# Moving the start addresses of a fused two-block transformer kernel's operand pools with small unused tiles

## The chip, the cores and the metric

The kernel runs on one core of a Trainium2 chip. The metric is the device time of one execution in microseconds (us); three timed executions are summed up by their median. One further execution was profiled, and the rows below are from that one. On-chip memory (SBUF) has 128 partitions; an address here is a byte offset within a partition, the same in all 128. TensorE (PE) takes two operands of a matmul from SBUF: the stationary one ("weights" of the array, loaded by a LDWEIGHTS that the profile lists under PEld) and the moving one, which streams through.

## What is computed

Two transformer blocks for one sequence of 512 tokens with 1024 features, all in float32. Cut to its outline:

```python
def first_block(x, c, ...):              # 2 layers, modulated by c
    for layer in range(2):
        mod = silu(c) @ ada_w[layer] + ada_b[layer]        # shift, scale, gate, twice
        h = rmsnorm(x, g) * (1 + scale_m) + shift_m
        y = gdn_mixer(h, ...) if layer == 0 else mla_mixer(h, ...)
        x = x + gate_m * y
        h = rmsnorm(x, g) * (1 + scale_f) + shift_f
        x = x + gate_f * ((silu(h @ w_gate) * (h @ w_up)) @ w_down)
    return rmsnorm(x, final_norm_g)

def second_block(x, ...):                # retention and window attention side by side
    h = rms_norm(x, ln1)
    proj = h @ w_in + b_in               # 1024 -> 6400 columns
    branch_a = (silu(rg) * head_norm(retention(rq, rk, rv))) @ w_ret_out
    branch_b = window_attention(aq, ak, av) @ w_attn_out
    x = x + (sigmoid(gate_a) * branch_a + sigmoid(gate_b) * branch_b) @ w_out
    x = x + swiglu(rms_norm(x, ln2))
    return rms_norm(x, lnf)
```

`gdn_mixer` is a chunked gated delta rule with 8 heads, `mla_mixer` is latent attention with 8 heads.

## The kernel before

**Products.** Nearly every large product is made three times in the format float32r, with both operands split into a high and a low part: high by high, low by high and high by low (`mm3`, L140 to L143). The stationary operand is a 128x128 piece of a weight matrix (`whi`, `wlo`), the moving one 512 or 256 tokens of an activation. In a few places (the values of attention and of retention) the roles are exchanged: the activation is loaded and the weights stream. A panel of weights (128 partitions x 1024 numbers) arrives by one DMA in `wraw`, ScalarE (ACT) copies its high part to `whi` (L566), and VectorE (DVE), in places GpSimd (POOL), subtracts to give `wlo` (L567). The stages run one after the other: the start, `gdn`, `ffn(0)`, `mla`, `ffn(1)`, `block2`, `ffn(2)`; `residual` closes each and prepares the first products of the next. Attention and the delta rule also use plain float32 matmuls, each of which shows as two records.

**Order.** PE's order is the order of the code, since PE is scheduled by hand (L335) with fillers between the chains (`Loom`). The other engines' queues are ordered by the scheduler of the language.

**Pools.** All tiles lie in pools that are stacked one behind the other, in the order in which they are opened. `Net.__init__` opens `cst` (constants), `sm` (small statistics), `adp`, `hp` (the split input of a stage, `hhi` and `hlo`, by `hpair`, L625) and `xp` (the residual stream). After `gdn`, `nm`, `wr` (`wraw`) and `wp` (`whi`, `wlo`) follow, and then each stage's own: `ffa` and `ffs` of `ffn` (`ah`, `al`, and `far`, `fsg`), `mla` of `mla`, `b2`, `b2c`, `b2s` of `block2`. The pools of `gdn` itself (`gh`, `gt` and others) are stacked from the other end. Two tiles hold more room than they use: `ones` (L377, 200 numbers more) and `lev` (L986, 24 more). In the built program `hp`, `xp`, `nm`, `wr`, `wp`, `ffa`, `ffs`, `mla` and `b2` begin at a multiple of 256 bytes, and so does every tile of 2048 or 4096 bytes in them. So each float32r matmul has its moving and its stationary operand at 0 mod 256, but for the 24 matmuls into `abps` of the start, whose stationary operand is 16 columns wide (64 bytes): the first and fifth three read it at 0, the other eighteen at 64, 128 and 192 mod 256. Elsewhere the start differs: `c_sq` (the identity and the masks) begins at 160 mod 256, `ones` at 128, and `rS`, the moving state of retention (L1469), at 96.

Of the kernel before, what the change touches and what calls it, by code (L numbers as in the profile page):

```python
# [12 lines left out]
F32 = mybir.dt.float32  # L13
# [7 lines left out]
P = 128  # L21
# [110 lines left out]


END = object()
Q3 = 0.65
LANES = 3
HALF = (slice(0, T // 2), slice(T // 2, T))
# [8 lines left out]
class Loom:  # L146
# [7 lines left out]
    def run(self, chains, filler, side=None, every=4):  # L154
        at = {g: self.t for g in chains}
        count, tries = 0, 0
        while at:
            ready = [g for g in at if at[g] <= self.t]
            for g in ready:
                if at[g] > self.t:  # L160
                    continue
                r = next(g, END)
                if r is END:
                    del at[g]
# [3 lines left out]
            if ready:  # L168
                continue
            c = next(filler, END)  # L170
            if c is END or c is None:
                self.t = max(self.t, min(at.values()))
# [151 lines left out]
class Net:  # L324
    def __init__(self, tc, I, es):
        self.tc, self.nc, self.I, self.es = tc, tc.nc, I, es
        self.cst = self.pool("cst", 1, es)
        self.sm = self.pool("sm", 4, es)
        self.adp = self.pool("adp", 1, es)
        self.hp = self.pool("hp", 8, es)  # L330
        self.xp = self.pool("xp", KD, es)
        self.pp = self.pool("pp", 3, es, space=PSUM)
        self.sp = self.pool("sp", 5, es, space=PSUM)
        self.wide, self.turn, self.lopool, self.behind = False, 0, False, None
        es.enter_context(tc.manual_schedule(engines={mybir.EngineType.PE}))  # L335

    def pool(self, name, bufs, es, **k):
        if k.get("space") is None:
            k["reuse_waits"] = "tile"
        return es.enter_context(self.tc.tile_pool(name=name, bufs=bufs, **k))  # L340

    def weights(self, es, n, **k):

# [3 lines left out]
    def first(self, gen, offset=300):  # L347

        while True:
            with self.tc.high_priority(offset=offset):  # L350
                r = next(gen, END)
            if r is END:
                return
# [252 lines left out]
    def stream(self, specs):  # L606

        nxt = specs[0][0]()
        for i, (_, h, done, *when) in enumerate(specs):
# [4 lines left out]
            for k, _ in enumerate(h(ps, wt) if callable(h) else self.proj(ps, wt, h)):  # L614
                if k == min(1, n - 1) and i + 1 < len(specs):
                    nxt = specs[i + 1][0]()
                if k < n - 1:
                    yield Q3
            done(ps)
            yield Q3  # L620

# [547 lines left out]
    def ffn(self, l, before, first, gate, norm, firsts, side=None):  # L1169
        nc, h = self.nc, before.h  # L1170
        wg, wu, wd = self.ffn_weights(l)
        with ExitStack() as es:
            fa, fs = self.pool("ffa", 8, es), self.pool("ffs", 2, es)
            sg, a = {}, None

            def gate_done(c):
                def done(ps):
                    sg[c] = fs.tile([P, T], F32, name="fsg")
                    if before.late:
                        nc.vector.tensor_tensor(sg[c], ps, before.row, op=ALU.mult)  # L1180
                        nc.scalar.activation(sg[c], sg[c], AF.Silu)  # L1181
                        nc.gpsimd.tensor_tensor(sg[c], sg[c], before.row, op=ALU.mult)  # L1182
                    else:
                        nc.scalar.activation(sg[c], ps, AF.Silu)
                return done

            def up_done(c, a):
                def done(ps):
                    ar = fs.tile([P, T], F32, name="far")
                    self.behind = nc.vector.tensor_tensor(ar, ps, sg.pop(c), op=ALU.mult).ins  # L1190
                    ah, al = fa.tile([P, T], F32R, name="ah"), fa.tile([P, T], F32R, name="al")
                    self.split(ah, al, ar)
                    a[0].append(ah)
                    a[1].append(al)
                return done
            specs = []
            for g, (lo, hi) in enumerate(FGROUPS):
                a = ([], [])
                for c in range(lo, hi):
                    specs += [(self.w(wg, c * P), h, gate_done(c)), (self.w(wu, c * P), h, up_done(c, a))]  # L1200
                if g < len(FGROUPS) - 1:
                    for n in range(KD):
                        specs.append((self.w(wd.rows(lo, hi), n * P), a, lambda ps, n=n: self.add_to_x(n, ps, gate)))
            for (_, _, done), ps in zip(specs, first):
                done(ps)
            for n, _ in enumerate(self.stream(specs[len(first):])):
                if side is not None and n % 5 == 0:
                    next(side, None)
            if side is not None:
                drain(side)  # L1210
                self.rope_tables(lambda name: self.nm.tile([P, T], F32, name=name, tag="sq", bufs=3))
            norm = norm()
            return norm, self.residual(wd.rows(lo, hi), a, gate, norm, firsts)
# [79 lines left out]
    def mla(self, h, first, gate, norm, firsts):  # L1293
        nc, I, sm = self.nc, self.I, self.sm
        scale = 192.0 ** -0.5
        with ExitStack() as es:
            mp = self.pool("mla", 37, es)
            t = lambda name: mp.tile([P, T], F32, name=name, tag="m")
            tr = lambda name: mp.tile([P, T], F32R, name=name, tag="m")
# [130 lines left out]
            f = fill()  # L1430
# [129 lines left out]
    def block2(self, before, first, norm, firsts):  # L1560
        nc, I, sm, h = self.nc, self.I, self.sm, before.h
        w = self.W("w_in_2")
        with ExitStack() as es:
            mp = self.pool("b2", 35, es)
            t = lambda name: mp.tile([P, T], F32, name=name, tag="m")
            tr = lambda name: mp.tile([P, T], F32R, name=name, tag="m")
# [172 lines left out]
            f = self.stream(specs)  # L1739
# [111 lines left out]
```

## Time and profile before

| | |
|---|---|
| median of three runs | 2292.67 us (2290.30 to 2297.39) |
| the profiled execution | 2289.49 us |
| its span, first to last instruction | 2287.7 us |
| PE busy | 2190.1 us, 96% |
| weight loads (PEld) busy | 1845.3 us, 81% |
| DVE, ACT, POOL busy | 1296.7, 875.5, 405.7 us |
| DMA, mean rate | 113 GB/s |

A busy time is the union of an engine's instructions. A matmul's record is longer than the time by which the next one follows it, since they are pipelined; so the cost of one in a stream is read from the starts of neighbours, not from its duration. The granted clock of TensorE has two levels here, full (2.4 GHz, written 1.00) and half (1.2 GHz, written 0.50); a value between them is a mixture within the stretch.

### The profile page before, as it was taken

What the parts mean: (1) busy time and instruction counts of PE and PEld (TensorE: products, weight loads), DVE (VectorE), ACT (ScalarE), POOL (GpSimd) and SP (SyncE); (2) the same over time, 40 slices, a digit from 0 to 9 for tenths busy, and PEclk for the clock granted to TensorE, in tenths of its full rate; (3) what the DMA queues carried; (4) which work ended last, traced back from release to release, by engine and by line L of the source; (5) the groups of instructions that cost most, each with busy time, mean ns of one, the idle gap of its engine ahead of it and who ended that gap; (6) DMA issues with size and microseconds to landing.
All of it is one profiled execution on the core that took longest, in us unless ns stands there. A gap on an engine that the chain in (4) does not pass through costs nothing.

```text
span 2287.7 us, 30713 instructions
## 1 busy us (share of the span) xinstructions
PE 2190.1 (96%) x11532; PEld 1845.3 (81%) x11532; DVE 1296.7 (57%) x2845; ACT 875.5 (38%) x1950; POOL 405.7 (18%) x331
## 2 busy tenths in 40 slices
PE   6999868899999999999999999999999999999998
PEld 4787767788888897679888888888778789888888
DVE  7888677577663356655433336665655655433334
ACT  4664355343222244434323234233544633322223
POOL 5345554120000031012000002212111002101011
PEclk7999888999999999999999999999999999999999
DMA  7233344248763313122332323433323141433332
GB/s 274 70 97 123 102 156 154 70 141 271 251 229 106 92 56 93 45 66 65 114 102 88 106 88 97 139 92 95 98 81 102 64 138 56 128 94 97 97 97 69
DMA packets 103236, 257.57 MB, mean 113 GB/s; under 512 B 26288, under 2 KB 36016, under 8 KB 103088
## 3 DMA queue, kind: packets, MB, share of 16 engines
q1 hardware_dynamic: 100496, 252.52, 35.3%
q10 hardware_dynamic: 2592, 3.10, 0.4%
q8 instruction: 90, 1.47, 0.3%
q14 instruction: 58, 0.48, 0.1%
HBM read 240.37 MB, written 8.91 MB: 109 GB/s over the span
## 4 chain that ended last, share of the span: by engine, by line
PE 78%; DVE 7%; POOL 2%; DMA 2%; issue 2%; ACT 1%; SPq 0%; DVEq 0%; POOLq 0%; ACTq 0%
PE ps L141 19%; PE ps L143 19%; PE ps L142 19%; PE ops L141 3%; PE ops L143 3%; PE ops L142 3%; PE first L141 1%; PE first L142 1%; PE first L143 1%; PE msc L1404 1%; PE mo_ps L1423 1%; POOL adaw L557 1%; PE msc L1403 1%; DVE wlo L567 1%; PE ssc L1516 1%
## 5 line engine op out<-in xcount | busy, mean ns | idle before, releaser
L566 ACT CAST whi<-wraw 128x512 fp32r<-128x512 f32 (+3 forms) x686 | 390.3, 605 | 924.9 <-PE ps L142 398.0
L141 PE MATMUL ps<-hhi,whi 128*128 128x512 f32 x1548 | 617.7, 399 | 3.6 <-ACT whi L566 1.8
L143 PE MATMUL ps<-hhi,wlo 128*128 128x512 f32 x1548 | 607.7, 393 | 5.5 <-POOL wlo L567 4.2
L142 PE MATMUL ps<-hlo,whi 128*128 128x512 f32 x1548 | 606.2, 392 | 0.8 <-DVE hlo L567 0.8
L567 DVE TENSOR_TENSOR wlo<-wraw,whi 128x512 fp32r<-128x512 f32 (+3 forms) x632 | 425.1, 700 | 170.1 <-ACT whi L566 169.7
L143 PEld LDWEIGHTS ps<-hhi,wlo 128*128 128x128 f32 x1548 | 292.7, 189 | 70.9 <-POOL wlo L567 5.1
L141 PEld LDWEIGHTS ps<-hhi,whi 128*128 128x128 f32 x1548 | 293.2, 189 | 68.2 <-issue 5.8
L142 PEld LDWEIGHTS ps<-hlo,whi 128*128 128x128 f32 x1548 | 293.1, 189 | 59.1 <-DVE hlo L567 1.1
L223 POOL TENSOR_TENSOR acc<-acc,sq 128x512 f32<-128x512 f32 x21 | 29.4, 1404 | 888.6 <-issue 636.2
L142 PE MATMUL ps<-al,whi 128*128 128x512 f32 x360 | 140.1, 389 | 0.0
L141 PE MATMUL ps<-ah,whi 128*128 128x512 f32 x360 | 140.1, 389 | 0.0
L143 PE MATMUL ps<-ah,wlo 128*128 128x512 f32 x360 | 140.1, 389 | 0.0
L1190 DVE TENSOR_TENSOR far<-ps,fsg 128x512 f32<-128x512 f32 x60 | 41.4, 691 | 172.3 <-PE ps L143 171.1
L141 PE MATMUL first<-hhi,whi 128*128 128x256 f32 (+1 forms) x336 | 102.1, 304 | 1.2 <-ACT whi L566 1.2
L143 PE MATMUL first<-hhi,wlo 128*128 128x256 f32 (+1 forms) x336 | 100.2, 298 | 1.0 <-POOL wlo L567 0.9
L142 PE MATMUL first<-hlo,whi 128*128 128x256 f32 (+1 forms) x336 | 100.2, 298 | 0.0
L567 POOL TENSOR_TENSOR wlo<-wraw,whi 128x512 fp32r<-128x512 f32 x54 | 78.3, 1469 | 94.9 <-ACT whi L566 94.8
L1182 POOL TENSOR_TENSOR fsg<-fsg,nrow 128x512 f32<-128x512 f32 x22 | 31.8, 1449 | 284.9 <-ACT fsg L1181 284.9
L141 PE MATMUL ops<-ah,whi 128*128 128x256 f32 (+1 forms) x252 | 81.5, 323 | 0.0
L142 PE MATMUL ops<-al,whi 128*128 128x256 f32 (+1 forms) x252 | 80.6, 320 | 0.0
L143 PE MATMUL ops<-ah,wlo 128*128 128x256 f32 (+1 forms) x252 | 80.6, 320 | 0.0
L560 DVE CUSTOM_DVE_ANT_0 adaw<-adaw,crow 128x1024 f32<-128x1024 f32 x56 | 68.3, 1222 | 19.5 <-DMA adaw<-in_ada_w_dram 19.3
(605 smaller groups left out, 3877.9 us busy)
## 6 DMA issues: line engine op xcount, KB each, us to landing
adaw<-in_ada_w_dram SPq DMA_DIRECT2D x96, 512.0 KB, 4.5
wraw<-in_ffn_w_gate_dram SPq DMA_DIRECT2D x44, 512.0 KB, 3.5
wraw<-in_ffn_w_up_dram SPq DMA_DIRECT2D x44, 512.0 KB, 3.6
wraw<-in_w_in_dram SPq DMA_DIRECT2D x42, 512.0 KB, 3.6
wraw<-in_gdn_w_in_dram SPq DMA_DIRECT2D x32, 512.0 KB, 3.7
wraw<-in_ffn_w_down_dram SPq DMA_DIRECT2D x32, 448.0 KB, 3.3
wraw<-in_w_ffn_gate_dram SPq DMA_DIRECT2D x22, 512.0 KB, 3.5
wraw<-in_w_ffn_up_dram SPq DMA_DIRECT2D x22, 512.0 KB, 3.5
```

The costliest lines, as they stand in the source:

```text
L141: nc.tensor.matmul(ps, whi, hhi, start=first, stop=False)
L142: nc.tensor.matmul(ps, whi, hlo, start=False, stop=False)
L143: nc.tensor.matmul(ps, wlo, hhi, start=False, stop=last)
L223: (nc.gpsimd if half is None else nc.vector).tensor_tensor(self.acc[i][:, cols], self.acc[i][:, cols], sq, op=ALU.add)
L557: nc.gpsimd.tensor_tensor(wt, wt, self.crow, op=ALU.mult)
L560: nc.vector.tensor_tensor_reduce(wt, wt, self.crow, 1.0, 0.0, ALU.mult, ALU.add, raw[:, k:k + 1])
L566: self.nc.scalar.copy(dst_hi, raw)
L567: (self.nc.gpsimd if pool else self.nc.vector).tensor_tensor(dst_lo, raw, dst_hi.bitcast(F32), op=ALU.subtract)
L1182: nc.gpsimd.tensor_tensor(sg[c], sg[c], before.row, op=ALU.mult)
L1190: self.behind = nc.vector.tensor_tensor(ar, ps, sg.pop(c), op=ALU.mult).ins
L1403: nc.tensor.matmul(ps[:, 0:nk], qn[hh][:, qs], kn[hh][:, 0:nk], start=True, stop=False)
L1404: nc.tensor.matmul(ps[:, 0:nk], qr[p][rows, qs], kr[rows, 0:nk], start=False, stop=True)
```

## The change

A function `gap(n)` opens a pool with one tile of n bytes per partition and lets POOL write its first number; nothing reads it. It is called with 64 bytes ahead of `hp`, 192 ahead of `xp`, 128 ahead of `ffa` in each `ffn`, and 32 ahead of `mla` and of `b2`. Seven tiny memsets are added, and the start addresses become these (bytes per partition, and modulo 256):

| pool | before | after |
|---|---|---|
| `hp` | 36864, 0 | 36928, 64 |
| `xp` | 69632, 0 | 69888, 0 |
| `nm` | 86016, 0 | 86272, 0 |
| `wr` and `wp` | 106496 and 114688, 0 | 106752 and 114944, 0 |
| `ffa` and `ffs` | 147456 and 180224, 0 | 147840 and 180608, 128 |
| `mla` and `b2` | 147456, 0 | 147744, 32 |

The pools of `gdn` stay where they are, at 0. The moving and the stationary operand of a float32r matmul then start 64 (input of a stage), 128 (`ffn`'s down product) or 32 bytes (`mla`, `b2`) apart modulo 256. Of 6816 such matmuls with 512 columns, 6720 have an operand that moved, and of 2472 with 256 columns 2280.

```diff
+GAPS = itertools.count()
@@ Net.__init__
         self.adp = self.pool("adp", 1, es)
+        self.gap(64, es)
         self.hp = self.pool("hp", 8, es)
+        self.gap(192, es)
         self.xp = self.pool("xp", KD, es)
@@
+    def gap(self, n, es):
+
+        t = self.pool(f"gap{next(GAPS)}", 1, es).tile([P, n // 4], F32, name="gap")
+        self.nc.gpsimd.memset(t[:, 0:1], 0.0)
@@ ffn
         with ExitStack() as es:
+            self.gap(128, es)
             fa, fs = self.pool("ffa", 8, es), self.pool("ffs", 2, es)
@@ mla
         with ExitStack() as es:
+            self.gap(32, es)
             mp = self.pool("mla", 37, es)
@@ block2
         with ExitStack() as es:
+            self.gap(32, es)
             mp = self.pool("b2", 35, es)
```

On PE, DVE, ACT and SP the instructions, their order and the engines that they wait for stay the same. On POOL the memsets come in at four places: two at the very start, and at the places shown here, with one more among the subtractions ahead of `ffn(2)`.

POOL before, at the end of `gdn` (`adaw` is a row of the modulation's weights, `acc` the sum of squares of the next norm):

```order
L883 TENSOR_TENSOR kraw<-kraw,gb 128x512 [waits PE_49,Pool_49]
L557 TENSOR_TENSOR adaw<-adaw,crow 128x1024 [waits DMAHW4_49,Activation_49]
L557 TENSOR_TENSOR adaw<-adaw,crow 128x1024 [waits DMAHW5_49,Activation_49]
L1302 MEMSET mask 128x384 [waits DMAHW0_49,DVE_49]
L557 TENSOR_TENSOR adaw<-adaw,crow 128x1024 [waits DMAHW6_49,Activation_49]
L223 TENSOR_TENSOR acc_3930<-acc_3930,sq 128x512 [waits Activation_49]
```

POOL after, at the same place:

```order
L1312 MEMSET mask 128x384 [waits DMAHW0_49,DVE_49]
L565 TENSOR_TENSOR adaw<-adaw,crow 128x1024 [waits DMAHW6_49,Activation_49]
L348 MEMSET gap 128x1 [waits DVE_49,PE_49]
L348 MEMSET gap 128x1 [waits Pool_49]
L224 TENSOR_TENSOR acc_3940<-acc_3940,sq 128x512 [waits Activation_49]
```

The gaps of `ffn(0)` and `mla` stand behind the last modulation row and ahead of the sums of squares.

POOL before, between `mla` and `ffn(1)` (`hlo` is the low part of the next stage's input):

```order
L567 TENSOR_TENSOR hlo_9257<-nt,hhi_9256 128x256 [waits Activation_49]
L567 TENSOR_TENSOR hlo_9270<-nt,hhi_9269 128x256 [waits Activation_49]
L567 TENSOR_TENSOR wlo<-wraw,whi 128x512 [waits Activation_49]
L567 TENSOR_TENSOR hlo_9283<-nt,hhi_9282 128x256 [waits Activation_49]
L567 TENSOR_TENSOR wlo<-wraw,whi 128x512 [waits DVE_49,DMAHW4_49,PE_49,Activation_49]
```

POOL after, at the same place:

```order
L575 TENSOR_TENSOR hlo_9278<-nt,hhi_9277 128x256 [waits Activation_49]
L575 TENSOR_TENSOR hlo_9291<-nt,hhi_9290 128x256 [waits Activation_49]
L348 MEMSET gap 128x1
L348 MEMSET gap 128x1 [waits Pool_49]
L575 TENSOR_TENSOR wlo<-wraw,whi 128x512 [waits Activation_49]
L575 TENSOR_TENSOR hlo_9304<-nt,hhi_9303 128x256 [waits Activation_49]
```

The gaps of `ffn(1)` and `block2` come in ahead of one subtraction of weights and one of the input.

## Rows read from the trace of the kernel before

**Rows 1.** The page: busy time, share of the span and instructions of each engine.

```profile
PE 2190.1 (96%) x11532; PEld 1845.3 (81%) x11532; DVE 1296.7 (57%) x2845; ACT 875.5 (38%) x1950; POOL 405.7 (18%) x331
```

**Rows 2.** The page: chain that ended last, shares by engine and by line.

```profile
PE 78%; DVE 7%; POOL 2%; DMA 2%; issue 2%; ACT 1%; SPq 0%; DVEq 0%; POOLq 0%; ACTq 0%
PE ps L141 19%; PE ps L143 19%; PE ps L142 19%; PE ops L141 3%; PE ops L143 3%; PE ops L142 3%; PE first L141 1%; PE first L142 1%; PE first L143 1%; PE msc L1404 1%; PE mo_ps L1423 1%; POOL adaw L557 1%; PE msc L1403 1%; DVE wlo L567 1%; PE ssc L1516 1%
```

**Rows 3.** Groups by form: count, busy us, mean ns, idle us before and its releasers.

```profile
L141 PE MATMUL ps<-hhi,whi 128*128 128x512 f32 x1548 | 617.7, 399 | 3.6 <-ACT whi L566 1.8 <-ACT hhi L566 1.8
L142 PE MATMUL ps<-al,whi 128*128 128x512 f32 x360 | 140.1, 389 | 0.0
L142 PEld LDWEIGHTS ps<-al,whi 128*128 128x128 f32 x360 | 67.6, 188 | 14.0
```

**Rows 4.** Timeline of PE in `ffn(0)`, 512 columns: start, duration in us, form.

```profile
699.66 0.39 PE L142 MATMUL ps<-al,whi 128*128 128x512 f32 x1
699.88 0.39 PE L143 MATMUL ps<-ah,wlo 128*128 128x512 f32 x1
...
707.82 0.39 PE L142 MATMUL ps<-al,whi 128*128 128x512 f32 x1
```

**Rows 5.** Timeline of PE at the end of `ffn(0)`, 256 columns.

```profile
805.62 0.28 PE L142 MATMUL ops<-al,whi 128*128 128x256 f32 x1
...
808.98 0.28 PE L143 MATMUL ops<-ah,wlo 128*128 128x256 f32 x1
```

**Rows 6.** Timeline of PE in the start, 512 columns, ahead of the first stream.

```profile
28.86 0.63 PE L141 MATMUL first<-hhi,whi 128*128 128x512 f32 x1
...
31.42 0.63 PE L141 MATMUL abps<-hhi,whi 128*16 128x512 f32 x1
```

**Rows 7.** Windows: stretch, length, busy (count) by engine, granted clock, DMA share, GB/s.

```profile
29.00:31.40 2.40, 2.40 (x7) 1.60 (x6) 2.37 (x3) 0.91 (x2) 2.40 (x3) 0.50 0.10 12
...
700.00:708.00 8.00, 8.00 (x37) 6.64 (x36) 3.90 (x6) 2.29 (x4) 0.00 (x0) 1.00 0.32 117
```

**Rows 8.** Timeline of PE later in the start, around matmuls into `abps`.

```profile
61.48 0.39 PE L143 MATMUL first<-hhi,wlo 128*128 128x512 f32 x1
61.71 0.40 PE L141 MATMUL abps<-hhi,whi 128*16 128x512 f32 x1
61.94 0.40 PE L142 MATMUL abps<-hlo,whi 128*16 128x512 f32 x1
62.18 0.39 PE L143 MATMUL abps<-hhi,wlo 128*16 128x512 f32 x1
62.40 0.39 PE L141 MATMUL first<-hhi,whi 128*128 128x512 f32 x1
```

**Rows 9.** Groups by form: float32 matmuls of retention, and DVE operations.

```profile
L1469 PE MATMUL ro<-rS,rx 128*128 128x256 f32 x24 | 7.1, 379 | 0.0
L1467 PE MATMUL rs<-rv,rkd 128*128 128x256 f32 x24 | 7.1, 379 | 0.0
...
L831 DVE TENSOR_TENSOR at<-gps,at 128x512 f32<-128x512 f32 x8 | 5.5, 682 | 0.4 <-POOL at L825 0.4
L794 DVE TENSOR_TENSOR at<-rps,c_sq 128x512 f32<-128x512 f32 x8 | 5.4, 678 | 0.0
```

**Rows 10.** Timeline of PE in `block2`, float32 matmuls (two records each).

```profile
1513.05 0.59 PE L1467 MATMUL rs<-rv,rkd 128*128 128x256 f32 x2
1513.48 0.59 PE L1469 MATMUL ro<-rS,rx 128*128 128x256 f32 x2
```

**Rows 11.** POOL: a group of small memsets, then its timeline after `gdn`.

```profile
L778 POOL MEMSET cz<- 128x1 f32 x24 | 2.2, 96 | 6.5 <-DVE hlo L485 6.5
...
386.22 2.35 POOL L557 TENSOR_TENSOR adaw<-adaw,crow 128x1024 f32<-128x1024 f32 x1
424.94 2.66 POOL L223 TENSOR_TENSOR acc<-acc,sq 128x512 f32<-128x512 f32 x2 [36.37 <-ACT sq L219]
```

**Rows 12.** Chain that ended last, in order of time: start us, us, step.

```profile
1048.21 1.06 POOL hlo L567
```

## The prediction

> **What bounds the kernel now.** I first read the busy times: PE works in 2190.1 of 2287.7 us, its weight loads in 81%, and no other engine is over 57% [rows 1]. The chain that ended last agrees: 78% of the span is PE, and most of that the three lines of `mm3`, the float32r products [rows 2]. The rest is mostly short float32 work and the gaps between stages. So a change of addresses matters if it changes the time from one float32r matmul to the next, its pitch. The groups give only the length of a record, 389 to 399 ns [rows 3], in which neighbours overlap; the pitch is read from starts. In a long undisturbed stretch of `ffn(0)` the matmul at 699.66 and the one 36 places on, at 707.82, are 8.16 us apart: 226.7 ns each [rows 4]. With 256 columns 28 steps take 808.98 - 805.62 = 3.36 us: 120.0 ns [rows 5]. At the full level of the clock, 2.4 GHz, 512 columns need 213.3 ns and 256 need 106.7; both pitches are 13.3 ns over that. This remainder, the same for a long and a short matmul, is the only thing that an address could give back, and it is what the sum below turns on.
>
> **Is the remainder a matter of addresses?** Before the change both operands start at 0 mod 256, so the suspicion is that the weight load and the moving stream meet in the same part of SBUF. Four readings bear on it.
>
> First, the two reads do not keep their distance. A load takes 188 ns [rows 3] and fetches 512 bytes of each partition; in the same time the moving stream, 2048 bytes in 226.7 ns [rows 4], goes on by 2048 x 188 / 226.7 = 1698 bytes. Their distance changes by about 1190 bytes during every load, over four times round a block of 256. A start that is 32, 64 or 128 bytes apart changes when they pass each other, not how often.
>
> Second, the weights of successive products lie 512 bytes apart in a panel, against moving tiles at multiples of 2048. So the pitch has been taken at four starting distances modulo 2048 already. All 36 steps fit 226.7 ns, since the rows between show 0.22 or 0.23 throughout [rows 4].
>
> Third, at half clock there is no remainder. From 28.86 to 31.42, six steps take 2.56 us, 426.7 ns each [rows 6], at a granted 0.50 [rows 7], and 512 columns at 1.2 GHz need 426.7. A collision of two reads that run at the same clock as the array would cost cycles at either level. A fixed step in the hand-over from one matmul to the next, hidden where the columns are slow, explains both.
>
> Fourth, there are a few starts off 0. The matmul at 61.48 runs while the next weights are read from 128 mod 256: the next start is 0.23 us later, as everywhere [rows 8]. Those weights are 16 columns wide, so this is a weak witness for wide ones. For plain float32, L1469 streams `rS` from 96 mod 256 against a load at 0, and L1467 `rv` from 0 against 0: both records are 379 ns [rows 9], and L1467's two passes take 1513.48 - 1513.05 = 0.43 us, 216 ns each for 256 columns [rows 10], which is 213.3 ns at half a column per array cycle plus 2.4. These read at half the rate of float32r, so they bound, they don't prove.
>
> **The change, part by part.** *Moved float32r operands.* 6720 matmuls with 512 columns and 2280 with 256, 9000 in all. The trace shows no wide float32r load at another distance, so I bound the price from both sides. Below: the remainder falls to the 2.4 ns of plain float32 [rows 10], 13.3 - 2.4 = 10.9 ns x 9000 = -98 us. Above: the slowest regular pitch of any float32r stream with off-0 operands, the `abps` matmuls at 61.71 to 62.18, 235 ns each [rows 8]: 235 - 226.7 = 8.3 ns x 9000 = +75 us. I take 0, by the first and third reading, and because it is the undisturbed float32r row nearest to what changes [rows 4]. Both ends stay for the range.
>
> *Moved float32 operands of `mla` and `block2`.* Both sides move by 32 together, so their distance stays; the transposes read the identity at 160 in any case. 0.
>
> *DVE and ACT.* They write and read the moved tiles at 32, 64 or 128. L794 reads its SBUF operand at 160 mod 256 and takes 678 ns, L831 the same kind of operation at 0 and takes 682 [rows 9]: 4 ns, and in the other direction. Off the path, since DVE is busy 57% [rows 1]. 0.
>
> *Seven memsets on POOL.* Memsets of 128x1 take 96 ns [rows 11]: 0.7 us of an engine that is busy 18%. The pair behind `gdn` waits for PE and DVE to have left the place; behind it stand the sums of squares. POOL is idle for 36.37 us between its last `adaw` and the first sum [rows 11], which covers both wait and memsets. The pair ahead of `ffn(1)` stands in front of two subtractions, and one `hlo` subtraction there is on the chain [rows 12]: 0.2 us at most. The one ahead of `ffn(2)` delays a `wlo` by 0.1 us. Together +0.3 us at most.
>
> *Other moves.* `xp`, `nm` and the weights shift by 256 and stay at 0 mod 256. The queues of PE, DVE, ACT and SP are as before, so no transfer starts in another order.
>
> The sum: 2289.5 (the profiled execution) + 0 + 0.3 = 2289.8 us. That execution was 3.2 us below the median, so on the scale of the median 2292.67 + 0.3 = 2293 us.
>
> **The rivals.** *Faster: the remainder is a collision after all, and 32 to 128 bytes separate the reads.* For it: the 13.3 ns are there in every float32r stream and not in float32 [rows 4, 5, 10]. Against: the drifting distance and the half clock. In full it gives 2293 - 98 = 2195 us; if only the 64 of the input helps or half of the remainder goes, 2240 to 2260. It counts from 0.8 ns a matmul (6.9 us over 9000).
>
> A page speaks for that rival: by the Trainium skill, "TensorE: Matmul & The Clock Gate", "Back-to-back issue gap", a warm matmul follows the one before after N / 2.4 + 2.5 ns. For 512 columns that is 215.7 ns, and the trace disagrees with 226.7 [rows 4]. If the missing 11 ns were due to the shared start, the sum would be about 99 us lower by it; the page names no address, so it gives a size and no reason.
>
> *Slower: a row that starts inside a block costs a further fetch.* A moving row of 2048 bytes from 32, 64 or 128 mod 256 touches nine blocks of 256 instead of eight. If the ninth delays the hand-over, each moved matmul pays, up to the +8.3 ns above: 2293 + 75 = 2368 us; at half of that 2330. For it: the `abps` rows are the only irregular ones, with operands off 0 [rows 8]. Against: in them the pitch is long only where one narrow load follows another (61.71 and 61.94), while 61.48 and 62.18, with an operand off 0 too, keep 0.22 to 0.23; that points at the 16 columns. And `rS` at 96 costs nothing [rows 9]. It decides from the same 0.8 ns a matmul. If it concerned only `mla` and `block2`, whose 32 is the least aligned start, it would be 1104 matmuls x 8.3 = +9 us, 2302 us.
>
> *The change does not act.* Weight distances drift as computed, so the new starts are only other phases; this is the forecast itself, 2293 us.
>
> **How the numbers follow.** No effect 0.74, collision removed 0.12, further fetch 0.14. A measurement of this kernel tells about 0.3% from no change, 6.9 us: 2286 to 2300. The range, 2255 to 2325, holds the first case and the smaller halves of both rivals (about 0.05 and 0.07), some 0.86 in all, and leaves out the large effects at both ends, about 0.14. Faster by over 0.3% gets 0.12, slower 0.14, within 0.74.
>
> **What would show it.** Right: the pitch in the down product of `ffn(0)` is again 226.7 ns for 512 columns and 120.0 for 256, the three `mm3` groups keep 389 to 399 ns, and PE's busy time stays within 5 us of 2190. Collision removed: that pitch falls toward 216, and the chain gets more of the other engines' steps. Further fetch: it rises, first where the start is 32. Apart from PE: the POOL pair behind `gdn` sits in an idle stretch; if the first sum of squares starts later against ACT's square, the cover was misread. The prediction is wrong if any of the three starts changes the pitch by 1 ns or more.

## The result and the profile after

The changed kernel takes 2306.91 us (median; 2302.70 to 2316.72) against 2292.67: ratio 1.0064, 95% interval 1.0045 to 1.0083. It is slower by 14.2 us, more than the 0.3% that a measurement of this kernel can tell. One of the seven executions took 2462.64 us at a granted clock of 0.839 instead of 0.98 and is left out of the range and the ratio; without it the median is 2306.1. The profiled execution took 2306.91 us with a span of 2305.1, so 17.4 us more than the profiled one of before.

Busy time by engine, on the page of the kernel after, against [rows 1]:

```profile
PE 2197.0 (95%) x11532; PEld 1834.5 (80%) x11532; DVE 1303.2 (57%) x2845; ACT 875.5 (38%) x1950; POOL 411.8 (18%) x338
```

PE has 6.9 us more of busy time for the same 11532 matmuls: 11.7 us more behind `gdn` and 4.9 less in the start and `gdn`, whose length varies (below). The seven instructions more on POOL are the memsets. The groups by form (count, busy us, mean ns, idle before) say which matmuls changed; the lines of the code have moved down by 1 to 11:

```profile
L142 PE MATMUL ps<-hhi,whi 128*128 128x512 f32 x1548 | 621.3, 401 | 3.9 <-ACT whi L574 2.2 <-ACT hhi L574 1.8
L143 PE MATMUL ps<-al,whi 128*128 128x512 f32 x360 | 142.0, 395 | 0.0
L142 PE MATMUL first<-hhi,whi 128*128 128x256 f32 x304 | 86.1, 283 | 1.2 <-ACT whi L574 1.2
```

Against [rows 3] the 512-column records grew from 399 to 401 ns (input at 64) and from 389 to 395 (`al` at 128). The 256-column record of `first` went the other way, from 289 to 283. The groups of before have its row, and that of the retention values, which stream over a loaded input:

```profile
L141 PE MATMUL first<-hhi,whi 128*128 128x256 f32 x304 | 87.8, 289 | 1.2 <-ACT whi L566 1.2
...
L141 PE MATMUL ps<-whi,hhi 128*128 128x256 f32 x128 | 36.5, 285 | 0.4 <-ACT nrow L316 0.4
```

Records overlap, so the pitch is read from starts, as in [rows 4, 5]. Timeline of PE after (start us, duration us, form), five stretches of 36 steps each, with the first and the last matmul shown. In order: moving operand at 64, 128 and 32 with 512 columns; moving at 64 with 256 columns; the loaded (stationary) operand at 64 with 256 columns.

```profile
728.30 0.39 PE L143 MATMUL ps<-hlo,whi 128*128 128x512 f32 x1
...
736.54 0.39 PE L143 MATMUL ps<-hlo,whi 128*128 128x512 f32 x1
...
701.02 0.39 PE L142 MATMUL ps<-ah,whi 128*128 128x512 f32 x1
...
709.39 0.40 PE L142 MATMUL ps<-ah,whi 128*128 128x512 f32 x1
...
1860.93 0.40 PE L144 MATMUL ps<-obh,wlo 128*128 128x512 f32 x1
...
1869.33 0.40 PE L144 MATMUL ps<-obh,wlo 128*128 128x512 f32 x1
...
1447.11 0.28 PE L142 MATMUL first<-hhi,whi 128*128 128x256 f32 x1
...
1451.35 0.28 PE L142 MATMUL first<-hhi,whi 128*128 128x256 f32 x1
...
1495.48 0.28 PE L142 MATMUL ps<-whi,hhi 128*128 128x256 f32 x1
...
1499.56 0.28 PE L142 MATMUL ps<-whi,hhi 128*128 128x256 f32 x1
```

The differences over 36 are 228.9, 232.5 and 233.3 ns where the same matmuls took 226.7 in the trace of before, and 117.8 and 113.3 ns where they took 120.0. Averaged over every pair of neighbours of like form that nothing interrupts (before: over all pairs of that width, all at distance 0):

| columns, operand, start mod 256 | pairs | pitch before, ns | pitch after, ns | sum, us |
|---|---|---|---|---|
| 512, moving, 64 | 4484 | 227.11 | 229.11 | +9.0 |
| 512, moving, 128 | 1329 | 227.11 | 232.37 | +7.0 |
| 512, moving, 32 | 570 | 227.11 | 233.10 | +3.4 |
| 256, moving, 64 | 885 | 119.86 | 117.02 | -2.5 |
| 256, moving, 128 | 477 | 119.86 | 118.59 | -0.6 |
| 256, moving, 32 | 376 | 119.86 | 116.85 | -1.1 |
| 256, loaded, 64 | 373 | 119.86 | 113.52 | -2.4 |
| 256, loaded, 32 | 84 | 119.86 | 118.25 | -0.1 |

Together +12.7 us, nearly all of the 14.2 between the medians. The profiled executions differ by more, 17.4 us, and 4.9 of it is there by the end of `gdn`. But so it is in kernels below that leave nearly all addresses of `gdn` alone: over seven of them the same matmul, the 1948th, starts between 435.3 and 441.9 us (before: 437.1, after: 442.0). That stage varies by itself from one execution to another. From the 1948th matmul to the last the two differ by 12.3 us, and the pairs behind it account for 11.7. So close a fit is partly chance: in the kernel `down_only` below the pairs give 8.4 us and that stretch 4.6.

One thing beside PE changed. POOL's timeline at the end of `gdn`, after:

```profile
431.52 0.25 POOL L348 MEMSET gap<- 128x1 f32 x2 [37.11 <-PE ops L144]
431.74 2.64 POOL L224 TENSOR_TENSOR acc<-acc,sq 128x512 f32<-128x512 f32 x2
```

ACT's square that the sum needs, before and after:

```profile
424.24 0.63 ACT L219 ACTIVATE sq<-xT 128x512 f32<-128x512 f32 x1 [0.65 <-DVE xT L642]
...
428.58 0.63 ACT L220 ACTIVATE sq<-xT 128x512 f32<-128x512 f32 x1 [0.65 <-DVE xT L650]
```

The first sum of squares no longer waits for ACT's square, as in [rows 11], but for the memsets ahead of it, and these for PE. It starts 6.8 us later than the 424.94 of [rows 11]: ACT's square is 4.3 us later, with the stage, and the sum starts 2.5 us behind the square's end instead of 0.1.

### The profile page after: what moved, and what is told of

It is laid out like the page before. It is cut to its first block, busy times and chain, and to the rows that moved or that the text cites. A ratio compares the mean times of both kernels' runs of the same rounds, so it can differ in the third digit from the quotient of the medians.

```text
span 2305.1 us, 30721 instructions
## 1 busy us (share of the span) xinstructions
PE 2197.0 (95%) x11532; PEld 1834.5 (80%) x11532; DVE 1303.2 (57%) x2845; ACT 875.5 (38%) x1950; POOL 411.8 (18%) x338
## 4 chain that ended last, share of the span: by engine, by line
PE 78%; DVE 8%; issue 2%; DMA 2%; ACT 1%; POOL 1%; SPq 1%; DVEq 0%; POOLq 0%; ACTq 0%
PE ps L142 19%; PE ps L144 19%; PE ps L143 19%; PE ops L142 3%; PE ops L143 3%; PE ops L144 3%; PE first L142 1%; PE first L143 1%; PE first L144 1%; PE msc L1414 1%; PE mo_ps L1433 1%; DVE wlo L575 1%; PE msc L1413 1%; PE ssc L1526 1%; DVE xp L867 1%
## 5 line engine op out<-in xcount | busy, mean ns | idle before, releaser
L144 PEld LDWEIGHTS ps<-ah,wlo 128*128 128x128 f32 x360 | 67.8, 188 | 15.9
```

The lines of the kernel that those rows point to most:

```text
L144: nc.tensor.matmul(ps, wlo, hhi, start=False, stop=last)
```

## The experiments

**1. Streams alone.** A kernel with nothing but `mm3` streams of 96 matmuls, over one copy of both operands, for every moving start in steps of 32 on four weight starts, in both widths (the code of this and of experiments 5 and 8 in outline).

```diff
+    for n, word in ((512, "wide"), (256, "half")):
+        for s in (0, 32, 64, 128):
+            for m in (0, 32, 64, 96, 128, 160, 192, 224):
+                stream(mov[:, m // 4:], wt[:, s // 4:], n)
```

> This kernel is no network: it streams float32r matmuls alone, in the order of the kernel (high by high, low by high, high by low, eight weights of 512 bytes, moving tiles 2048 bytes apart), 96 for each pair of a moving start (0 to 224 mod 256 in steps of 32) and a weight start (0, 32, 64, 128), with 512 and with 256 columns. Its output is a copy of one sum and not the network's. Theory A, the time from one matmul to the next depends on the two starts: at moving 32, 64, 128 on weights at 0 it gives about 233, 229, 232 ns for 512 columns and 117, 117, 119 for 256, as in the trace of the changed kernel, against 226.7 and 120 for 0 on 0; other pairs lie between 226 and 241. Rival B, the rise in the changed kernel comes from its surroundings (other engines' accesses to shifted tiles, weights at 256 mod 512) and not from the operands' starts: every pair gives 226.7 and 120 here. If only the distance between the starts counts, 64 on 64 and 128 on 128 are as 0 on 0.

The view of one tile gives the first and the last start of a line; a line has 32 of a stream's 96 matmuls, so the difference is 93 steps. The names say width, moving start and weight start (a is 0, b 32, c 64, e 128, f 160, g 192). View of eight tiles, PE only (count, duration ns min/median/max, first to last start us, form):

```profile
L24 PE MATMUL widebona<-mov,wt x32: 393/396/399, 38.0 to 59.7; 128*128 128x512 f32 x32
...
L24 PE MATMUL widecona<-mov,wt x32: 388/388/398, 60.4 to 81.7; 128*128 128x512 f32 x32
...
L24 PE MATMUL wideeona<-mov,wt x32: 392/395/398, 104.8 to 126.5; 128*128 128x512 f32 x32
...
L24 PE MATMUL wideconc<-mov,wt x32: 389/389/395, 417.5 to 438.6; 128*128 128x512 f32 x32
...
L24 PE MATMUL halfaona<-mov,wt x32: 278/283/283, 729.2 to 740.3; 128*128 128x256 f32 x32
...
L24 PE MATMUL halfcona<-mov,wt x32: 280/280/283, 752.0 to 763.0; 128*128 128x256 f32 x32
...
L24 PE MATMUL halfgona<-mov,wt x32: 276/276/286, 797.5 to 808.1; 128*128 128x256 f32 x32
...
L24 PE MATMUL halfaonc<-mov,wt x32: 281/281/281, 910.3 to 921.3; 128*128 128x256 f32 x32
```

21.7, 21.3 and 21.7 us over 93 steps are 233, 229 and 233 ns: the network's three pitches within 1 ns, with no other engine at work and no network. And 64 on 64 is 21.1 us, 227 ns, as 0 on 0. So with 512 columns what counts is the distance between the starts, not either start. Over the last 72 steps of each stream, with d = moving start minus weight start modulo 256:

| d | 0 | 32 | 64 | 96 | 128 | 160 | 192 | 224 |
|---|---|---|---|---|---|---|---|---|
| 512 columns, ns | 226.7 | 233.3 | 228.9 | 233.3 | 233.3 | 234.3 | 233.3 | 233.3 |
| 256 columns, ns | 120.0 | 117.8 | 117.8 | 120.0 | 118.7 | 117.4 | 113.3 | 118.3 |

For 512 columns all 32 pairs follow d. For 256 columns 30 do; the two others are 0 on 64 (117.8, not 113.3) and 32 on 128 (118.7, not 117.4). With 512 columns the kernel before stood at the best distance of the eight. With 256 columns it stood at one of the worst two. The further runs show that for 256 columns the distance alone does not decide (experiments 5 and 8).

**2 to 4. One part of the change each.** `input_only` keeps the gaps of 64 and 192 ahead of `hp` and `xp`, `down_only` that of 128 in `ffn`, `mix_only` those of 32 in `mla` and `block2`.

```diff
 input_only:  +self.gap(64, es)    +self.gap(192, es)
 down_only:   +self.gap(128, es)
 mix_only:    +self.gap(32, es)    # in mla and in block2
```

> Only the gaps ahead of hp (64) and xp (192): a stage's input hhi, hlo at 64 mod 256, all else at 0. Theory A: the 512-column matmuls on hhi go from 227.1 to 229.1 ns, 4484 x 2.0 = +9 us; the 256-column ones fall, 885 x 2.9 and, as loads, 373 x 6.4, together -5 us; sum +4 us, 0.2%, plus what the gdn stage adds beside its streams, some 4 us: ratio 1.002 to 1.004. Rival B (surroundings): no change of the pitch, ratio 1.000.

> Only the gap of 128 ahead of ffa and ffs: ah, al at 128 mod 256. Theory A: 1329 matmuls with 512 columns at 232.4 instead of 227 ns, +7 us, 477 with 256 columns 1.3 ns less, -0.6 us; sum +6.5 us, ratio 1.003. Rival B: ratio 1.000.

> Only the gaps of 32 ahead of mla and b2: operands of the two mixers at 32 mod 256. Theory A: 570 matmuls with 512 columns at 233.1 instead of 227 ns, +3.5 us; 376 + 84 with 256 columns 3 and 2 ns less, -1.3 us; sum +2 us, ratio 1.001, hardly to be told from 1. Rival B: 1.000. A rival for the rest, slower copies between tiles at 32 mod 64 for the rotations, would add more than 3 us in the two mixers.

| part | median, us | ratio | 95% interval | pitch 512, ns | pitch 256, ns | loads, ns |
|---|---|---|---|---|---|---|
| `input_only` | 2297.23 | 1.0011 | 0.9998 to 1.0025 | 229.15 | 117.24 | 113.49 |
| `down_only` | 2300.80 | 1.0029 | 1.0016 to 1.0041 | 233.29 | 118.68 | |
| `mix_only` | 2295.50 | 1.0004 | 0.9991 to 1.0016 | 233.25 | 116.70 | 118.10 |

Each part changes the pitch of its own matmuls as the whole change did, within 1 ns (the most at 128 bytes: 233.29 here, 232.37 in the whole, at the same distance), and leaves the others. In the groups of `down_only`, for instance, only the second row moved against [rows 3]:

```profile
L142 PE MATMUL ps<-hhi,whi 128*128 128x512 f32 x1548 | 616.9, 399 | 3.9 <-ACT whi L572 2.1 <-ACT hhi L572 1.8
L143 PE MATMUL ps<-al,whi 128*128 128x512 f32 x360 | 142.2, 395 | 0.0
```

Only `down_only` is slower beyond its interval; `input_only` stayed under the 1.002 to 1.004 that was expected. The input has the most matmuls, and nearly cancels: its 512-column ones lose 9 us and its 256-column ones give back 5. The product of the three ratios is 1.0044, the whole 1.0064 with 1.0045 to 1.0083. The intervals overlap, so no interaction of the parts is shown or needed.

**5. Finer starts and narrower weights.** Streams alone again, moving starts in steps of 4 over weights at 0, and weights of 16, 32 and 64 columns.

```diff
-            for m in (0, 32, ..., 224):
+            for m in (0, 4, 8, ..., 252, 256, 320, 384, 448):   # 35 starts
+        for c in (16, 32, 64, 128):   # columns of weights
```

> Streams alone again, 72 matmuls for each case; the output is a copy of one sum and not the network's. Weights always start at 0; the moving tiles start at 0 to 252 in steps of 4 to 32 and at 256, 320, 384, 448; and, for starts 0, 64, 128, 192, the weights are 16, 32, 64 or 128 columns wide. Theory A, the weight load and the moving stream hinder each other by where they meet: the pitch repeats with 256 (256 as 0, 320 as 64), changes between steps of 32 as well or in steps of a line, and shrinks toward 213 to 216 ns (512 columns) when fewer weight columns are loaded. Rival B, the 13.3 ns over 213.3 are a fixed step of the hand-over, to which the start adds a phase: narrow weights give the same 226.7 at 0, and no less anywhere.

View of four tiles (24 of a stream's 72 matmuls in a line, so 69 steps); the three letters are the digits of the moving start, a for 0 to j for 9: 0, 4, 20 and 256.

```profile
L26 PE MATMUL widefullaaa<-mov,wt x24: 389/389/397, 215.5 to 231.2; 128*128 128x512 f32 x24
...
L26 PE MATMUL widefullaae<-mov,wt x24: 394/401/403, 231.9 to 248.3; 128*128 128x512 f32 x24
...
L26 PE MATMUL widefullaca<-mov,wt x24: 394/404/404, 298.9 to 315.4; 128*128 128x512 f32 x24
...
L26 PE MATMUL widefullcfg<-mov,wt x24: 389/389/395, 734.6 to 750.3; 128*128 128x512 f32 x24
```

0 and 256 take 15.7 us over 69 steps, 4 takes 16.4 and 20 takes 16.5. In steady state: 226.7, 238.1, 240.0 and again 226.7 ns. The period of 256 holds at 320, 384 and 448 as well, which repeat 64, 128 and 192 in both widths. Four bytes are enough to change the pitch, by 11.4 ns. Of all starts only 0, 240 and 256 give 226.7 with 512 columns, and none gives less. With 256 columns the range is 113.3 to 123.3. Narrower weights do not shrink the remainder in step with their bytes: at distance 0, 16, 32 and 64 columns of weights give 228.9, 231.7 and 230.0 ns under 512 moving ones (128: 226.7), and 116.7, 117.8 and 113.3 under 256 (128: 120.0). A remainder that grew with the bytes loaded would fall to a fraction with 16 columns, so it is no plain sum of single collisions. A hand-over whose step depends on where the two reads stand to each other would fit, but no run shows what the step is.

Two of the starts repeat experiment 1 and take another pitch: 32 on 0 with 256 columns takes 116.7 ns here and 117.8 there, 128 on 0 with 512 columns 232.2 and 233.3. The last 36 steps of 32 on 0, first in experiment 1, then here:

```profile
747.65 0.28 PE L26 MATMUL halfbona<-mov,wt 128*128 128x256 f32 x1
...
751.89 0.28 PE L26 MATMUL halfbona<-mov,wt 128*128 128x256 f32 x1
...
973.53 0.28 PE L28 MATMUL halffulladc<-mov,wt 128*128 128x256 f32 x1
...
977.73 0.28 PE L28 MATMUL halffulladc<-mov,wt 128*128 128x256 f32 x1
```

4.24 us against 4.20. Each stream repeats a pattern of its own from start to start: 118, 119, 116 ns in the one, 116, 118, 120, 113 in the other. So the two starts do not fix the pitch alone; a stream can settle into more than one rhythm. Which of the other differences between the two kernels (what ran ahead, the room around the tiles) chooses it was not tried.

**6. The same start with the distance put back.** A gap of 64 ahead of `hp` alone, and none behind, moves all the pools behind it by 64, the weights too, so that from `ffn(0)` on all float32r operands start at 64 and the distance is 0.

```diff
+        self.gap(64, es)      # ahead of hp, and no gap behind it
         self.hp = self.pool("hp", 8, es)
```

> One gap of 64 ahead of hp and none behind it: from the end of gdn on, operands and weights all start at 64 mod 256; in gdn the weights stay at 0 under an input at 64. Theory A by distance: the streams after gdn keep 226.7 and 120 ns (distance 0), ratio 1.000 to 1.001 (the gdn stage has some 600 matmuls of 512 columns at distance 64, 2.2 ns each, +1.4 us). Rival, the start by itself counts: as input and down product at 64, 512 columns at 229 ns, 6100 x 2 = +12 us, ratio 1.005.

2293.31 us, ratio 0.9998 (0.9988 to 1.0009). The pitch is 227.03 ns with 512 columns and 119.84 with 256, as before, where the distance is 0. Elsewhere it is not: 650 pairs in `gdn`, with the input at 64 on weights at 0, have 229.38, and at its end 168 pairs of 256 columns, which stream from 0 on weights at 64, have 114.5. A moving row from 64 costs nothing by itself. In the groups of this kernel the first row is that of before:

```profile
L142 PE MATMUL ps<-hhi,whi 128*128 128x512 f32 x1548 | 616.3, 398 | 3.3 <-ACT hhi L573 1.8 <-ACT whi L573 1.5
```

**7. A distance for each width.** If 512 columns are best at distance 0 and 256 columns are not, then the weight panels that only 256-column products use may start elsewhere. The kernel before, with these panels at 64, and with the retention values' weights, which stream over a loaded input at 0, at 192.

```diff
-        hi = self.wp.tile([P, kc, n], F32R, name="whi", tag="whi")
+        hi = self.wp.tile([P, 1024 + 64], F32R, name="whi", tag="whi")[:, at:at + kc * n]...
@@ residual: get(n)
+            self.shift = 64 if n >= KD - nh else 0     # at = shift // 4
@@ values: weights()
+                        self.shift = 192
```

> The kernel before, with one edit: the weight panels that are used by 256-column products alone (the last four columns of residual and the first products of the next stage) start at 64 mod 256 under operands at 0, distance 192, and the retention's value weights, which stream, at 192 over a loaded input at 0, distance 192 as well; all 512-column products stay at distance 0. Theory A by distance, from the map of streams: 2376 matmuls with 256 columns at 113.3 instead of 120.0 ns, -15.8 us, ratio 0.993; 512 columns unchanged. Rival: the products of 256 columns wait for the norms and weights around them, so the time comes back as waiting: ratio 0.997 to 1.000.

2284.81 us, ratio 0.9964 (0.9953 to 0.9976): faster than both kernels. The 512-column pitch stayed (227.13 ns), but the 256-column ones fell to 115.95 (1879 pairs) and 116.68 (373 pairs) only, not to 113.3. That is 7.3 + 1.2 = 8.5 us, against 8.3 by the ratio. The size was off since the exceptions of experiment 1 were passed over: 0 on 64, the panels' case, is one of them, at 117.8. In the network the panels' pitch is not one number: 114.5 ns at the end of `gdn`, 115.1 in `first` and 117.3 in the down product of `ffn`, all with 0 on 64. For the values, 192 on 0, the stream alone does give 113.3, and the network takes 3.4 ns more.

**8. All weight starts for 256 columns.** Streams alone, moving at 0, weights from 0 to 252 in steps of 4, in two orders of the same products, each stream behind 24 matmuls of 512 columns.

```diff
+    for word, cross in (("plain", False), ("woven", True)):   # k runs inside, or outside
+        for c in range(0, 256, 4):
+            stream(mov, wt[:, c // 4:], 256)
```

> Streams alone, the output is a copy of one sum and not the network's. The moving tiles start at 0 and the weights at 0 to 252 in steps of 4; each case is 72 products of 256 columns behind 24 of 512 columns with both at 0, once with the weights in a row (plain) and once with three weights in turn for one moving tile (woven), as the first products of a stage are. Theory A by distance alone: a weight start of s is a distance of 256 - s, so s = 64, 68, 184 and 220 give 113.3 ns as the distances 192, 188, 72 and 36 did, in both orders. Rival C, the stream can settle into one of several rhythms at one distance, by what ran before: some s give 113.3 in one order and 116 to 120 in the other, and s = 64 lies near the 116 of the kernel with halves at 192.

View of three tiles, with the digits of the weight start as letters (76 in both orders, and 64; 69 steps):

```profile
L25 PE MATMUL plainahg<-mov,wt x24: 276/276/281, 288.2 to 296.0; 128*128 128x256 f32 x24
...
L25 PE MATMUL wovenahg<-mov,wt x24: 276/276/281, 1184.3 to 1192.1; 128*128 128x256 f32 x24
...
L25 PE MATMUL plainage<-mov,wt x24: 281/281/281, 246.2 to 254.4; 128*128 128x256 f32 x24
```

In steady state 113.3, 113.3 and 117.8 ns. The two orders agree within 0.1 ns at all 64 starts, so this order doesn't matter. But 0 on 128 takes 120.0 ns here and 118.6 in experiment 1, so again the starts alone do not fix the pitch. Neither does the distance: 112 on 0 takes 113.3 (experiment 5), 0 on 144, the same distance modulo 256, 120.0. The four weight starts that were expected to give 113.3 (64, 68, 184 and 220) give 117.8, 118.4, 117.8 and 120.7; for the last three the letters of experiment 5 had been misread as well. Only 76, 88 and 180 reach 113.3; 204 is the worst with 123.3; most lie between 116.7 and 120.1.

**9 to 11. The three best starts in the network.** As experiment 7, with the panels at 76, 88 and 180, and the values' weights at 72, 36 and 188.

```diff
-            self.shift = 64 if n >= KD - nh else 0
+            self.shift = 76 if n >= KD - nh else 0     # 88, 180
-                        self.shift = 192
+                        self.shift = 72                # 36, 188
```

> The kernel before, with the weight panels that only 256-column products use beginning at byte 76 (the 512-column ones at 0) and the retention value weights, which stream over a loaded input at 0, at 72. Theory D, the rhythm follows from the two starts alone: the stream alone gave 113.33 ns with weights at 76, and with the moving operand at 72, in either order, so 1,879 matmuls go from 119.9 to 113.3 ns and 373 from 119.9 to 113.5, 14.8 us less, ratio 0.9935. Theory E, the rhythm also hangs on what was issued ahead of the stream (with weights at 64 the stream alone gave 117.8 and the network's matmuls 115.95 ns): somewhere between 113 and 120 ns, a ratio between 0.9935 and 1.000, and the three kernels of this call differ from one another and from 113.3.

> The same with the panels at byte 88 and the value weights at 36. The stream alone gave 113.33 ns for either. Theory D: 113.3 and 113.5 ns, ratio 0.9935, the same time as with 76 and 72. Theory E: another pitch than with 76 and 72, between 113 and 120 ns, ratio between 0.9935 and 1.000.

> The same with the panels at byte 180 and the value weights at 188. The stream alone gave 113.33 ns for either. Theory D: 113.3 and 113.5 ns, ratio 0.9935, the same time as the other two. Theory E: another pitch than theirs, between 113 and 120 ns, ratio between 0.9935 and 1.000.

The expectations hold an error: for 72, 36 and 188 as moving starts experiment 5 shows 118.3, 121.5 and 120.0 ns, not 113.3. The letters of its tiles had been misread here too.

| panels, values | median, us | ratio | 95% interval | pitch with the panels, ns (alone) | pitch with the values, ns (alone) |
|---|---|---|---|---|---|
| 76, 72 | 2285.02 | 0.9948 | 0.9935 to 0.9961 | 113.66 (113.3) | 120.95 (118.3) |
| 88, 36 | 2280.59 | 0.9930 | 0.9915 to 0.9946 | 114.19 (113.3) | 121.06 (121.5) |
| 180, 188 | 2278.48 | 0.9927 | 0.9915 to 0.9938 | 114.96 (113.3) | 118.47 (120.0) |

All three beat the kernel before, by 10 to 17 us. The main term came out as the streams alone said, within 0.3 to 1.6 ns: in the groups of the kernel with 88 and 36 the row of `first` is at 281 ns, against 289 before and 283 after, while the row of the values, 287, is above the 285 of before:

```profile
L141 PE MATMUL first<-hhi,whi 128*128 128x256 f32 x304 | 85.5, 281 | 0.0
...
L141 PE MATMUL ps<-whi,hhi 128*128 128x256 f32 x128 | 36.7, 287 | 0.4 <-ACT nrow L316 0.4
```

So theory D holds for the panels to a first approximation, but not to the tenth of a nanosecond: the pitches differ from one another and from 113.3, as theory E says, and with the values the network is up to 2.7 ns off the stream alone, in either direction. The pitches account for 11.1 us with 76, 10.4 with 88 and 9.7 with 180, against 10.2, 14.6 and 16.8 between the medians. The 4 to 7 us that the last two gained beyond their pitches are not explained.

**12. A repeat by mistake.** The next run was to have the values' weights at 112, where the stream alone takes 113.3 ns.

```diff
 (no line differs from experiment 9: panels at 76, values at 72)
```

> Panels of the 256-column products at byte 76 as before, the retention value weights, which stream over a loaded input at 0, now at 112. For 72, 36 and 188 the stream alone had been misread: it shows 118.3, 121.5 and 120.0 ns there, not 113.3; for 112 it shows 113.33. The network's matmuls gave 120.95, 121.06 and 118.47 at 72, 36 and 188. Theory D, the rhythm follows from the two starts alone: the 373 matmuls with values go from 119.9 to 113.3 to 113.7 ns, the others keep 113.7, together 14.2 us under the kernel before, ratio 0.994. Theory E, the rhythm also hangs on what was issued ahead: the values take between 116 and 121 ns, together 10.5 to 13 us under, ratio 0.9945 to 0.9955; the pitch of the values tells the two apart, not the ratio.

The start was left at 72, so the run is a repetition of experiment 9: 2283.14 us, ratio 0.9959 (0.9944 to 0.9974), pitches 113.63 and 120.85 ns against 113.66 and 120.95. It shows how well a pitch repeats from one chip to another (0.1 ns), and how much less well the time does (0.9948 and 0.9959). Values at 112 weren't tried.

## Why the prediction was right in its range and wrong in its forecast

The range of 2255 to 2325 us holds 2306.91. The likeliest case, no measurable change with 0.74, did not come; slower by over 0.3% had 0.14. That the range held owes something to luck: it was wide enough for half of either rival, but neither rival's mechanism came as it was told, and the change is what two effects of opposite sign left over.

*What bounds the kernel.* Right. The pitch of the float32r matmuls was by far the most of what the addresses changed, and the time followed it: +12.7 us by the pitches, +14.2 by the medians.

*"I take 0" for the moved float32r operands.* This is the step that failed. The bounds, -98 and +75 us, held the true value, but the value was not 0. It was +12.7: +19.4 from 512 columns, -6.7 from 256. The text had set its own test, 1 ns at any of the three starts, and all three went past it: +2.0, +5.3 and +6.0 ns with 512 columns. PE's busy time left its 5 us too, with +6.9.

*First reading, the drifting distance.* That the distance between the two reads drifts is arithmetic and stands. That a start therefore can't matter was the mistake. Modulo 256 the distance at which a load begins is the same for every matmul of a stream, and with 512 columns the pitch depends on it (experiment 1).

*Second reading.* Right, and it could have been a warning. The four distances modulo 2048 that the trace held were all 0 modulo 256, that is, one case and not four. A trace of one distance can't tell that distances don't matter.

*Third reading, a fixed step in the hand-over.* Half borne out. The remainder doesn't shrink in step with the bytes loaded (experiment 5), so it isn't a plain sum of collisions. But it isn't fixed: 13.3 ns at distance 0 and up to 26.7 (240.0 - 213.3) at others. At half clock there is no remainder at other distances either, as the kernel after shows in two stretches with a granted clock of 0.50, at distance 64 with 512 columns and at 128 with 256:

```profile
29.55 0.63 PE L142 MATMUL first<-hhi,whi 128*128 128x512 f32 x1
...
31.68 0.63 PE L144 MATMUL first<-hhi,wlo 128*128 128x512 f32 x1
...
834.59 0.41 PE L143 MATMUL ops<-al,whi 128*128 128x256 f32 x1
...
837.15 0.41 PE L143 MATMUL ops<-al,whi 128*128 128x256 f32 x1
```

The windows of the two stretches (columns as in [rows 7]; the clock is the third number from the end):

```profile
29.55:31.68 2.13, 2.13 (x6) 1.65 (x5) 2.10 (x3) 0.54 (x1) 2.13 (x3) 0.50 0.00 0
...
834.59:837.15 2.56, 2.56 (x13) 2.56 (x13) 2.53 (x7) 2.41 (x6) 0.59 (x1) 0.50 0.69 204
```

Five steps of 426 ns and twelve of 213.3 ns: 512 and 256 columns at 1.2 GHz. So at these two distances the price is there at the full clock alone. A pitch without a remainder at half clock therefore said nothing against a price at full clock, which is where the reading went wrong.

*Fourth reading.* The prediction called the 16 columns a weak witness and the float32 rows a bound, and that was the right weight for them. They said nothing about wide float32r loads. The 0.43 us of [rows 10] are 215 ns a pass and not 216, which moves the lower bound by a few us and nothing else.

*The faster rival, a collision removed.* Wrong for 512 columns: no start tried is better than distance 0, and the layout of before had it. For 256 columns it has a grain of truth, since distance 0 is among the worse; the change gave 6.7 us there. The Trainium skill, "TensorE: Matmul & The Clock Gate", section "Back-to-back issue gap", gives N / 2.4 + 2.5 ns as the gap of an isolated matmul, by estimate 215.7 ns for 512 columns and 109.2 for 256, and says that a stream of weight loads and matmuls departs from it. The trace does, upward: the lowest pitches in any run here were 226.7 and 113.3.

*The slower rival, a ninth block.* The sign was right and the mechanism wrong. Experiment 6 has rows that start at 64 and touch nine blocks, and their pitch is 227.03 ns. The price of a pair depends on the distance, and 32 costs a little more than 128 and much more than 64, which no count of blocks gives.

*POOL.* The size, +0.3 us, is not resolved by the runs, but the reading of the cover was wrong, in the way the prediction had named. The memsets behind `gdn` wait for PE beyond the time at which ACT's square is there, so the first sum of squares starts 2.5 us behind the square, in the kernel after and in `down_only`, instead of 0.1. What follows hides most of it: from the 1921st to the 1961st matmul PE loses 1.5 us against before in either kernel. Of the kernels without a memset there six lose 1.4 or 1.5, `mix_only` 2.5 and `input_only` nothing. More than 1 or 2 us can't be put down to it.

*DVE, ACT and float32.* Nothing shows there: DVE's busy time went from 1296.7 to 1303.2 us, off the path, and ACT's stayed at 875.5.

## What to carry to other kernels

Where a kernel is bound by streams of float32r matmuls with a new weight load each, the start addresses of the two operands modulo 256 are a tuning parameter worth some tenths of a per cent: keep them equal for 512 columns, and try several starts in the network itself for 256, where neither the distance nor a table of bare streams fixes the pitch. A trace in which all operands share one alignment can't say what another alignment costs; a kernel of bare streams can, and its pitches carried over within 1 ns for 512 columns, but only within about 4 for 256. And a matmul's length in a group of records moves with the pitch but not by as much or as little (`first`: 6 ns shorter for 2.8 ns of pitch), so read the pitch from starts.

## What the runs showed of the hardware that was not expected

- With 512 columns the pitch of float32r matmuls that each load 128 columns of weights follows the distance between the moving and the stationary start modulo 256, down to 4 bytes and within about 1 ns: 226.7 ns (0) to 240.0 (20 and 196).
- At a granted 0.50 two distances had no price: 512 columns took 426 ns at 64, as at 0 before the change, and 256 took 213.3 at 128.
- For 256 columns the range is 113.3 to 123.3 ns, and 0 on 0, the best for 512, gives 120.0. The distance doesn't decide there (112 on 0: 113.3, 0 on 144: 120.0), and the same two starts can settle into different rhythms (32 on 0: 117.8 and 116.7; 0 on 128: 118.6 and 120.0).
- A small load need not be cheaper: with 16 columns of weights instead of 128 the 512-column pitch at distance 0 rose from 226.7 to 228.9 ns, while the 256-column one fell from 120.0 to 116.7.
- What chooses the rhythm, and so what sets the two exceptions among the 32 pairs of 256 columns and the difference between a stream alone and the same starts in the network (0 on 64: 117.8 alone, 113.5 with a loaded input in the network after, 115.95 with the panels of experiment 7), stays open.
